# A planner that orders four engines: durations by kind, hops by engine, and dense weights in quarter rings

## The chip, the cores and the metric

One Trainium2 chip, one core. The metric is the device time of one execution in microseconds (us). The engines are named as the profile names them: PE (TensorE), DVE (VectorE), ACT (ScalarE), POOL (GpSimd) and SP (SyncE, which issues most transfers).

## What is computed

One layer of a diffusion backbone over 256 latent tokens and 256 context tokens of 2048 channels, in fp32. Cut to what matters:

```python
h  = modulate(rmsnorm(x, norm1_w), sh1, sc1)          # latent, 256 x 2048
hc = modulate(rmsnorm(ctx, norm1_w), csh1, csc1)      # context, 256 x 2048
rw, cv, z, ab, gt = split(h @ w_in)                   # the combined input projection; hc likewise
fa = rwkv_features(rw, grid_shift(rw), ...)           # 16 heads of 64: decay and iclr by low-rank products
out_a = [prefix_scan(rwkv7_scan, context, latent, s0, reverse) for both directions]
fb = gdn_features(cv, ab, conv_w, ...)                # 8 heads of 128: conv of 5 tokens, l2norm
out_b = [prefix_scan(gdn_chunked, context, latent, s0, reverse) for both directions]
m = sigmoid(g_a) * (o_a @ p_a) + sigmoid(g_b) * (o_b @ p_b)
x = x + gt1 * (m @ w_out)
x = x + gt2 * swiglu(modulate(rmsnorm(x, norm2_w), sh2, sc2), ...)
return rmsnorm(x, final_norm_w)
```

Both recurrences are computed in chunks of 64 tokens. Each needs the inverse of a triangular 64 x 64 matrix for each chunk, and a chain of small products that carries the state from chunk to chunk (8 steps for a pair of RWKV heads, context and latent, both directions at once; 4 steps of two chunks for a GDN head).

## The kernel before, in words

**Stages.** Until 133 us of the span the modulation vectors and norms are made. From 133 to 1368 us runs the woven stage: the input projection together with both recurrences. From 1368 us to the end the merge and the FFN run as plain products (`load_w`, `gemm`, L345 to L376). The change touches the woven stage alone.

**Dense products.** The input projection is 86 products of 128 output columns (`products`, L1061). Each takes its inputs in 16 blocks k of 128 channels, and each block is three matmuls, because fp32 is split in two parts: hi weight by hi input (`mm<-hxh,whi`), hi by lo (`mm<-hxl,whi`), lo by hi (`mm<-hxh,wlo`). They are 512 columns wide where the context is needed too, else 256. `cast` (L1041) loads the weights into two raw halves of 128 x 8 x 128 (512 KB each, tag wraw, 3 buffers), ACT makes the hi part of a quarter (`whi`, 128 x 512), DVE subtracts to get the lo part (`wlo`), and these go into a fixed ring of four quarters (L1037 to L1039). The ring's quarter is written again when the product before has read it.

**RWKV pairs.** `lowrank` (L733) makes decay and iclr inputs of the 8 pairs: for each pair four products `s<-lin,wraw`, whose outputs ACT takes through a sigmoid (`lo<-s`) and stores. For each two pairs it loads 384 KB of low-rank weights (`lora`) into a buffer of the tag wraw. Then for each pair come `prepare` (L765), `grams` (L847, whose helper `four` at L855 halves the planned cost of its products), `inverse` (L897), `values` (L908) and `scan` (L923). A step of the scan is a product `s<-VX,LA..`, a copy to R by ACT, a product `s<-R,Tx` with the inverse, copies to VX by ACT, and a product `s<-VX,KB` whose result DVE multiplies into VX for the next step.

**GDN heads.** `features`, `tokens`, `decays`, `head_grams`, `head_inverse` and `head_scan` (L1238 to L1377) for each of 8 heads. The inverse passes between engines and through memory: DVE ends a triangle, SP stores it (`tscr<-arena`), loads it back in another layout (`T<-tscr`), and DVE transposes it in blocks (`Tx<-T`). In the scan, DVE makes Vn from a product and the state St from the next. Beside the heads, `ada_rest` (L1449) makes the remaining modulation vectors on DVE: 180 steps `aw<-aw,ck`, each 128 x 512.

**What sets the order.** All pieces above are generators that yield operations. The planner (`Weave`, L170 to L266) runs them against a model of the engines while the program is built, and the order in which it takes operations is the order of the instructions on PE, DVE, ACT and POOL. It always takes the operation that can start first by its model, and between equals the one with the lower rank (scans low, dense products 900). The model is the table `LAT` (L30) and `Lane` (L112): a planned duration for each operation, `own` between two operations of a piece on the same engine, `hop` where the piece changes engines, `turn` where PE changes between dense (split) and other products, and `dma` behind a transfer. SP isn't planned; its transfers stand in the order in which the pieces ask for them, and each waits for its buffer in that order. Instructions of the planned engines all have line L143 in the profile, transfers L154.

Of the kernel before, what the change touches and what calls it, by code (L numbers as in the profile page):

```python
# [18 lines left out]
P = 128  # L19
D = 2048  # L20
KT = D // P
T = 256
# [7 lines left out]
LAT = dict(dma=2.4, v=1.0, s=1.0, hop=0.5, own=0.13, grp=32, crank=-1, cg=4, turn=0.09)  # L30
# [70 lines left out]

HOP = LAT['hop']


class Op:


    def __init__(self, lane, cost, call, split=False):
        self.lane, self.cost, self.call, self.split = lane, cost, call, split


class Lane:  # L112


    def __init__(self, engine, fixed, each, own):
        self.engine, self.fixed, self.each, self.own = engine, fixed, each, own

    def __getattr__(self, name):

        def op(out, *a, **k):  # L120
            if name == "preload_act_table_set":
                return Op(self, 1.3, lambda: self.engine.preload_act_table_set(out))
            if name == "dma_start":
                return Op(self, 0.6 if self.each > 0.002 else 0.06, lambda: self.engine.dma_start(out, *a))
            n = int(np.prod(out.shape[1:]))
            split = name == "matmul" and a[0].dtype == F32R
            if name == "transpose" and len(a) == 2:
                cost = 0.109
            elif split:
                cost = 0.0065 + 0.000443 * n  # L130
            elif name == "matmul":
                rows, m = a[0].shape[0], out.shape[0]
                if rows < 64:
                    cost = 0.009 if n <= 16 else 0.0125
                elif rows == 64:
                    cost = max(0.066, 0.027 + 0.0008 * n)
                elif rows < P or m == P:
                    cost = 0.0054 + 0.00167 * n
                else:
                    cost = 0.107  # L140
            else:
                cost = self.fixed + self.each * n
            return Op(self, cost, lambda: getattr(self.engine, name)(out, *a, **k), split)  # L143
        return op
# [24 lines left out]

class Weave:  # L170

    def __init__(self):
        self.work, self.free, self.done, self.now, self.split = [], {}, {}, 0.0, True

    def add(self, rank, gen, at=None):
        now = self.now  # L180
        w = [rank, gen, None, now if at is None else at, None, None]
        self.work.append(w)
        self.step(w, None)
        self.now = now

    def step(self, w, value):

        while True:
            self.now = w[3]
            try:  # L190
                x = w[1].send(value)
# [4 lines left out]
            if isinstance(x, float):  # L196
                w[3] += x
            w[5] = x if not isinstance(x, Op) else [x]
# [4 lines left out]
    def there(self, w):  # L203
        x = w[5]
# [4 lines left out]
    def take(self, w):  # L209
        x = w[5]  # L210
        w[5] = None
        if isinstance(x, tuple) and isinstance(x[0], Banks):
            w[3] = max([w[3]] + [b.free.pop(0) for b in x])
            return [b.tile() for b in x]
        if isinstance(x, Banks):
            w[3] = max(w[3], x.free.pop(0))
            return x.tile()
        w[3] = max(w[3], self.done[x] + HOP)

    def ready(self, *name):  # L220
        self.done[name] = self.now

    def release(self, banks):
        banks.free.append(self.now)

    def run(self):
        while self.work:
            for w in list(self.work):
                if w[5] is not None and not isinstance(w[5], (list, float)) and self.there(w):
                    self.step(w, self.take(w))  # L230
            best = None
            for w in self.work:
                if isinstance(w[5], float):
                    key = (w[3], w[0])
                    if best is None or key < best[0]:
                        best = (key, w, None)
                elif isinstance(w[5], list):
                    lane = w[5][0].lane
                    at = w[3] + (0.0 if w[4] is None else lane.own if w[4] is lane else HOP)
                    key = (max(self.free.get(lane, 0.0), at), w[0])  # L240
                    if best is None or key < best[0]:
                        best = (key, w, lane)
            if best is None:
                if any(w[5] is not None and not isinstance(w[5], (list, float)) and self.there(w) for w in self.work):
                    continue
                assert not self.work, [w[5] for w in self.work]
                return
            (start, _), w, lane = best
            if lane is None:
                w[5] = None  # L250
                assert w[3] < 1e5, [x[5] for x in self.work]
                self.step(w, None)
                continue
            ops, rest, w[4] = w[5], None, lane
            if lane is self.tensor:
                ops, rest = ops[:LAT['grp']], ops[LAT['grp']:]
                if ops[0].split != self.split:
                    start += LAT["turn"]
                self.split = ops[0].split
            w[5] = rest or None  # L260
            got = [o.call() for o in ops]
            w[3] = self.free[lane] = start + sum(o.cost for o in ops)
            if rest:
                w[4] = None
            else:
# [3 lines left out]
def emit(ctx: ExitStack, tc, A, out, dbg=None):  # L269
# [6 lines left out]
    e, v, s = Lane(E, 0.027, 0.00083, 0.0), Lane(V, 0.07 * LAT["v"], 0.00104 * LAT["v"], LAT["own"]), Lane(S, 0.06 * LAT["s"], 0.00086 * LAT["s"], LAT["own"])  # L276
    g = Lane(G, 0.06, 0.0024, LAT["own"])
# [441 lines left out]

    for b in (pib, mmb, psb, psb, mmb, pab):  # L720
# [4 lines left out]
    def lowrank_out(p, j, ps, so):  # L725
# [4 lines left out]
        if j == 3:  # L730
            weave.ready("lowrank", p)

    def lowrank():  # L733
# [17 lines left out]
        for p in range(NPAIR):  # L751
# [95 lines left out]
    def grams(p, d):  # L847
# [7 lines left out]
        def four(ops):  # L855
            for o in ops:
# [868 lines left out]
```

## Time and profile before

| | us |
|---|---|
| median of 3 runs | 2311.51 (2311.5 to 2324.71) |
| profiled execution, its own time | 2311.51 |
| its span, first instruction to last | 2309.7 |
| ahead of the woven stage | 133 |
| woven stage: low-rank products / RWKV scans / GDN heads / last dense products | 129 / 688 / 300 / 118 |
| merge and FFN | 941.7 |

The mean granted TensorE clock was 0.974. In a row of the profile, "a<-b,c" are the tiles written and read; "x4" after a shape counts instructions; what stands in square brackets or behind an arrow at the end is the idle time before it and what ended it. Dense matmuls overlap each other, so the distance between two starts (the pitch), not the duration, is what one costs.

### The profile page before, as it was taken

How to read it: one execution, taken by the hardware profiler on the slowest of the kernel's cores; microseconds unless marked ns; L12 is line 12 of the kernel's file. 1: busy time of each engine (PE TensorE's matmuls, PEld its weight loads, DVE VectorE, ACT ScalarE, POOL GpSimd, SP SyncE). 2: the span in 40 equal slices, each digit the busy share in tenths (PEclk: the TensorE clock that was granted, in tenths of full speed). 3: DMA queues.
4: the chain of work that ended last, by engine and by line, in shares of the span. 5: the costliest groups of instructions: out<-in, count | busy, mean ns of one | idle time of the engine just before them, and what ended most of it. 6: DMA issues, size and time to landing. Idle time of an engine off the chain costs nothing.

```text
span 2309.7 us, 54901 instructions
## 1 busy us (share of the span) xinstructions
PE 2176.4 (94%) x22904; PEld 1910.7 (83%) x22904; DVE 1553.1 (67%) x3242; ACT 1105.0 (48%) x2057; POOL 110.0 (5%) x183
## 2 busy tenths in 40 slices
PE   7988999999999999888888999999999999999998
PEld 4766677776778677776777989999999999999997
DVE  3447588887787558889988755765666666555554
ACT  3246554543555556544555446554444444444443
POOL 0000000000000001111111003000000000000000
PEclk9999999999999999999899999999999999999999
DMA  9956543443434236666667666663777776566665
GB/s 384 403 146 193 166 114 107 116 110 93 127 100 120 80 94 215 197 176 205 204 192 218 186 205 206 211 224 108 243 239 237 238 241 230 195 189 194 196 194 166
DMA packets 232728, 430.77 MB, mean 187 GB/s; under 512 B 114848, under 2 KB 130208, under 8 KB 228128
## 3 DMA queue, kind: packets, MB, share of 16 engines
q1 hardware_dynamic: 204832, 351.77, 48.8%
q0 software_dynamic: 13824, 50.34, 7.2%
q10 hardware_dynamic: 13824, 25.17, 3.3%
q8 instruction: 179, 2.93, 0.5%
q14 instruction: 69, 0.57, 0.1%
HBM read 401.44 MB, written 25.77 MB: 185 GB/s over the span
## 4 chain that ended last, share of the span: by engine, by line
PE 66%; DVE 15%; DMA 9%; ACT 5%; issue 4%; SPq 1%; ACTq 0%; DVEq 0%; POOL 0%; POOLq 0%
PE mm L143 17%; PE mm L376 12%; PE mm L374 12%; PE mm L375 12%; PE s L143 5%; DVE arena L143 4%; PE pa L143 3%; DVE aw L143 2%; DVE wlo L143 2%; DMA tscr<-arena 2%; PE pi L143 2%; DMA wr<-wgu 2%; PE mm L467 1%; DMA wraw<-wgu 1%; DVE wlo L365 1%
## 5 line engine op out<-in xcount | busy, mean ns | idle before, releaser
L365 DVE TENSOR_TENSOR wlo<-wraw,whi 128x1024 fp32r<-128x1024 f32 x328 | 393.3, 1199 | 340.6 <-ACT whi L364 339.7
L364 ACT CAST whi<-wraw 128x1024 fp32r<-128x1024 f32 x328 | 337.6, 1029 | 457.8 <-PE mm L375 403.0
L143 PE MATMUL mm<-hxh,wlo 128*128 128x256 f32 (+1 forms) x1376 | 470.1, 342 | 10.7 <-DVE wlo L143 10.1
L143 PE MATMUL mm<-hxh,whi 128*128 128x256 f32 (+1 forms) x1376 | 466.4, 339 | 4.8 <-ACT whi L143 4.6
L143 PE MATMUL mm<-hxl,whi 128*128 128x256 f32 (+1 forms) x1376 | 464.4, 338 | 0.0
L376 PE MATMUL mm<-hfh,wlo 128*128 128x256 f32 x1344 | 372.4, 277 | 1.3 <-DVE wlo L365 1.3
L374 PE MATMUL mm<-hfh,whi 128*128 128x256 f32 x1344 | 371.2, 276 | 0.0
L375 PE MATMUL mm<-hfl,whi 128*128 128x256 f32 x1344 | 371.2, 276 | 0.0
L143 PEld LDWEIGHTS mm<-hxh,wlo 128*128 128x128 f32 x1376 | 265.3, 193 | 39.3 <-DVE wlo L143 13.8
L143 DVE TENSOR_TENSOR wlo<-wraw,whi 128x512 fp32r<-128x512 f32 x344 | 238.0, 696 | 80.8 <-ACT whi L143 77.9
L143 PEld LDWEIGHTS mm<-hxh,whi 128*128 128x128 f32 x1376 | 266.1, 193 | 31.0 <-ACT whi L143 7.0
L143 PEld LDWEIGHTS mm<-hxl,whi 128*128 128x128 f32 x1376 | 265.8, 193 | 26.9 <-issue 5.0
L143 ACT CAST whi<-wraw 128x512 fp32r<-128x512 f32 x344 | 209.1, 617 | 137.9 <-PE mm L143 112.9
L376 PEld LDWEIGHTS mm<-hfh,wlo 128*128 128x128 f32 x1344 | 252.4, 188 | 2.9 <-DVE wlo L365 2.7
L374 PEld LDWEIGHTS mm<-hfh,whi 128*128 128x128 f32 x1344 | 252.5, 188 | 0.0
L375 PEld LDWEIGHTS mm<-hfl,whi 128*128 128x128 f32 x1344 | 252.5, 188 | 0.0
L374 PE MATMUL mm<-za,whi 128*128 128x256 f32 x512 | 141.5, 276 | 0.0
L376 PE MATMUL mm<-za,wlo 128*128 128x256 f32 x512 | 141.3, 276 | 0.0
L375 PE MATMUL mm<-za,whi 128*128 128x256 f32 x512 | 141.3, 276 | 0.0
L143 DVE SCALAR_TENSOR_TENSOR aw<-aw,ck 128x512 f32<-128x512 f32 x180 | 132.5, 749 | 3.3 <-DMA aw<-ada_rest 3.0
L143 DVE TENSOR_TENSOR arena<-arena 128x512 f32<-128x512 f32 (+17 forms) x522 | 121.3, 234 | 17.0 <-DMA arena<-scr 7.8
L375 PEld LDWEIGHTS mm<-za,whi 128*128 128x128 f32 x512 | 96.1, 188 | 0.0
(333 smaller groups left out, 3916.0 us busy)
## 6 DMA issues: line engine op xcount, KB each, us to landing
wraw<-w SPq DMA_DIRECT2D x172, 512.0 KB, 4.1
wraw<-wgu SPq DMA_DIRECT2D x168, 512.0 KB, 4.5
aw<-ada_rest POOLq DMA_DIRECT2D x96, 512.0 KB, 4.6
aw<-ada_first SPq DMA_DIRECT2D x32, 1024.0 KB, 12.0
wraw<-wdn SPq DMA_DIRECT2D x64, 448.0 KB, 3.7
wraw<-wout SPq DMA_DIRECT2D x32, 512.0 KB, 4.5
aw<-ada_gt ACTq DMA_DIRECT2D x64, 256.0 KB, 5.0
wraw<-wdn SPq DMA_DIRECT2D x32, 512.0 KB, 3.6
```

The costliest lines, as they stand in the source:

```text
L143: return Op(self, cost, lambda: getattr(self.engine, name)(out, *a, **k), split)
L364: S.copy(hi[:, c, :M], raw[:, c, :M])
L365: V.tensor_sub(lo[:, c, :M], raw[:, c, :M], hi[:, c, :M].bitcast(F32))
L374: E.matmul(ps, hi, Xh[:, k, :n], start=first and i == 0, stop=False)
L375: E.matmul(ps, hi, Xl[:, k, :n], start=False, stop=False)
L376: E.matmul(ps, lo, Xh[:, k, :n], start=False, stop=last and i == len(wt) - 1)
L467: E.matmul(ps[32 * g:32 * g + 32, 0:P], ckr[:, k].rearrange("p a b -> p (a b)"), aws[e, c][:, i, g], start=k == 0, stop=k == KT - 1)
```

## The change

**Planner.** A matmul's planned cost now depends on its kind (`product`), that of other engines on the operation and its operands (`cost`). Hops go by engine: PE 0.215, DVE 0.135, ACT 0.15, POOL 0.1, plus 0.1 of slack each, in place of 0.5 for all. `own` falls from 0.13 to 0.09 (0 on PE), `dma` rises from 2.4 to 3.1. PE is charged 0.14 for leaving the full array, 0.2 for coming back and 0.14 between two small kinds, where 0.09 stood for each change; 0.1 for a dense product after a pause; DVE and ACT 0.08 when the output's partitions change. A piece is an object that knows its own engine, so what it makes ready or releases counts from the end of its operation plus that engine's hop.

**Weights.** The rings of raw, hi and lo weights are quarters (128 x 4 x 128), handed out and given back one by one: 6 raw, 4 hi, 4 lo. `fetch` asks for a quarter (256 KB) when a raw one is free, `cast` splits it; each is a piece of its own. Until the low-rank products are done, two of the raw quarters are set aside for their weights, which are loaded per pair (192 KB) and two pairs ahead. `scan(0)` waits until the low-rank outputs of the last pair are done.

The core of the diff:

```diff
-LAT = dict(dma=2.4, v=1.0, s=1.0, hop=0.5, own=0.13, grp=32, crank=-1, cg=4, turn=0.09)
+LAT = dict(dma=3.1, v=1.0, s=1.0, hop=dict(e=0.215, v=0.135, s=0.15, g=0.1), slack=0.1, own=0.09, grp=32, crank=-1, cg=4, into=0.14, back=0.2, cross=0.14, stay=0.0)
...
+    def product(self, out, a):
+        n, rows, m = int(np.prod(out.shape[1:])), a[0].shape[0], int(np.prod(a[0].shape[1:]))
+        if a[0].dtype == F32R:
+            return 0.0065 + 0.000443 * n, "full"
+        if rows >= 96 and m == P:
+            return max(0.219, 0.012 + n * 4 / 2400), "full"
+        mode = (rows, m)
+        if rows < 64:
+            return 0.0165, mode
+        if rows == 64:
+            return (0.064 if n > 64 else 0.048) if m < P else 0.02 + n * 4 / 2400, mode
+        return (0.06 if m < 64 else 0.058), mode
...
+    def at(self, lane):
+        if self.lane is None:
+            return max(self.end, self.seen)
+        return max(self.end + (lane.own if lane is self.lane else self.lane.hop), self.seen)
+
+    def shown(self):
+        return max(self.end + (self.lane.hop if self.lane else 0.0), self.seen)
...
+    def turn(self, mode):
+        return 0.0 if mode == self.mode else LAT["back"] if mode == "full" else LAT["into"] if self.mode == "full" else LAT["cross"]
...
+    raws, his, los = quarters("wraw", 3, F32), Ring(quarters("whi", 2, F32R)), Ring(quarters("wlo", 2, F32R))
+    raws, spare = Ring(raws[:4]), raws[4:]
...
+    def lora(p):
+        landed["lora", p] = weave.now + dq(spare[p % 2][:96], A["lora"][p // 2, :, 4 * (p % 2):4 * (p % 2) + 4])
...
-            if p % 2 == 0:
-                w = wp.tile([P, 8, P], F32, tag="wraw", name="wraw", bufs=3)
-                yield dq(w[:96], A["lora"][p // 2])
+            if p == 0:
+                for i in range(2):
+                    lora(i)
+            yield max(0.0, landed["lora", p] - weave.now)
+            w = spare[p % 2]
             for j in (0, 2, 1, 3):
                 ps = yield psb
-                yield e.matmul(ps, w[:96, 4 * (p % 2) + j], lin[:, j], start=True, stop=True)
+                yield e.matmul(ps, w[:96, j], lin[:, j], start=True, stop=True)
                 weave.add(2, lowrank_out(p, j, ps, out[j]))
+            if p + 2 < NPAIR:
+                lora(p + 2)
+        raws.put(*spare)
...
-        if p:
-            yield "scan", p - 1
+        yield ("scan", p - 1) if p else ("lowrank", NPAIR - 1)
...
+    def fetch(src, i):
+
+        for q in range(NQ):
+            raw = yield raws
+            landed[i, q] = raw, weave.now + dq(raw, src[:, CG * q:CG * q + CG, :])
+            weave.ready("asked", i, q)
+            yield 0.0
+
+    def cast(i):
+
+        for q in range(NQ):
+            yield "asked", i, q
+            raw, at = landed.pop((i, q))
+            yield max(0.0, at - weave.now)
+            hi = yield his
+            yield s.copy(hi, raw)
+            lo = yield los
+            yield v.tensor_sub(lo, raw, hi.bitcast(F32))
+            raws.put(raw)
+            casts[i, q] = hi, lo
+            weave.ready("cast", i, q)
```

**Where instructions move.** PE, low-rank products of the later pairs (`s<-lin,wraw`; `pa<-C,arena` are transposes of the first pair; the rows `mm` are dense). Before:

```order
L143 MATMUL pa<-C,arena 128x128 x4
L143 MATMUL mm<-hxl,whi 128x512
L143 MATMUL s<-lin,wraw 128x512 x2
L143 MATMUL mm<-hxh,wlo 128x512
L143 MATMUL s<-lin,wraw 128x512 x6
L143 MATMUL mm<-hxh,whi 128x512
```

And now:

```order
L158 MATMUL s<-lin,wraw 128x512 x2
L158 MATMUL mm<-hxh,wlo 128x512
L158 MATMUL s<-lin,wraw 128x512 x2
L158 MATMUL pa<-LAl,arena 64x128 x16
L158 MATMUL s<-lin,wraw 128x512 x2
L158 MATMUL mm<-hxh,whi 128x512
L158 MATMUL s<-lin,wraw 128x512 x2
L158 MATMUL mm<-hxl,whi 128x512
L158 MATMUL s<-lin,wraw 128x512 x2
L158 MATMUL pa<-C,arena 128x128 x4
```

The products of six and eight in a row are taken apart into twos, with one other row between.

PE, a step of an RWKV scan, from the product with VX to the product with R. Before:

```order
L143 MATMUL s<-VX,LAc 64x64 x4
L143 MATMUL mm<-hxh,wlo 128x512
L143 MATMUL mm<-hxh,whi 128x512
L143 MATMUL mm<-hxl,whi 128x512
L143 MATMUL mm<-hxh,wlo 128x512
L143 MATMUL mm<-hxh,whi 128x512
L143 MATMUL s<-R_6133,Tx 64x64 x4
```

And now:

```order
L158 MATMUL s<-VX,LAl 64x64 x4
L158 MATMUL mm<-hxh,whi 128x512
L158 MATMUL mm<-hxl,whi 128x512
L158 MATMUL mm<-hxh,wlo 128x512
L158 MATMUL s<-R_6244,Tx 64x64 x4
L158 MATMUL s<-VX,C 64x128 x2
L158 MATMUL s<-LAl,VX 64x64 x4
```

Three dense matmuls stand where five stood, and the products that don't depend on R follow it directly.

DVE, third GDN head, from the last row of the triangle (`arena<-arena 64x15`) to the transpose of what was loaded back (`Tx<-T`). Before:

```order
L143 TENSOR_TENSOR arena<-arena 64x15 x2
L143 COPY arow<-pa 128x256
L143 SCALAR_TENSOR_TENSOR arena<-arena 128x256
L143 TENSOR_TENSOR arena<-s,arena 128x128 x2
L143 TENSOR_TENSOR mod<-pa,PR 128x4 x2
L143 TENSOR_TENSOR Qe<-Qe,arena 128x256
L143 TENSOR_TENSOR keg<-pa,egc 128x512
L143 TENSOR_TENSOR arena<-arena 128x256
L143 TENSOR_TENSOR kta<-pa,eta 128x512
L143 SCALAR_TENSOR_TENSOR arena<-arena,PR 128x256
L143 STREAM_TRANSPOSE Tx<-T_11590 128x256
```

And now:

```order
L158 TENSOR_TENSOR arena<-arena 64x15
L158 TENSOR_TENSOR keg<-pa,egc 128x512
L158 TENSOR_TENSOR wlo<-wraw,whi 128x512
L158 TENSOR_TENSOR kta<-pa,eta 128x512
L158 SCALAR_TENSOR_TENSOR aw<-aw,ck 128x512
L158 TENSOR_TENSOR keg<-pa,egc 128x512
L158 TENSOR_TENSOR wlo<-wraw,whi 128x512
L158 TENSOR_TENSOR kta<-pa,eta 128x512
L158 SCALAR_TENSOR_TENSOR aw<-aw,ck 128x512 x3
L158 TENSOR_TENSOR wlo<-wraw,whi 128x512
L158 TENSOR_TENSOR Qe<-Qe,arena 128x256
L158 SCALAR_TENSOR_TENSOR aw<-aw,ck 128x512
L158 STREAM_TRANSPOSE Tx<-T_11684 128x256
```

Between the two stand three `wlo`, five `aw` and five other instructions where eleven, most of them shorter, stood.

More of the change, by code (lines that the diff above doesn't have):

```diff
@@ L275, in emit @@
     dq = Loads(Q)
[L276 to L277 removed]
+    e, v, s, g = (Lane(x, fixed, each, LAT["own"], LAT["hop"][n]) for x, fixed, each, n in
+                  ((E, 0.0, 0.0, "e"), (V, 0.07, 0.00104, "v"), (S, 0.06, 0.0009, "s"), (G, 0.06, 0.0022, "g")))
+    e.own = 0.0
     ent = ctx.enter_context
@@ L713, in turn, with quarters @@
         weave.release(pab)
+    CG = LAT['cg']
+    NQ = KT // CG
+    def quarters(tag, n, dtype):
+        return [t[:, k:k + CG] for t in [wp.tile([P, 8, P], dtype, tag=tag, name=tag, bufs=n) for _ in range(n)] for k in range(0, 8, CG)]
+    raws, his, los = quarters("wraw", 3, F32), Ring(quarters("whi", 2, F32R)), Ring(quarters("wlo", 2, F32R))
+    raws, spare = Ring(raws[:4]), raws[4:]
     for b in (pib, mmb, psb, psb, mmb, pab):
@@ L1035, in gate_out, with weights @@
         Q.dma_start(gts_[j], g)
[L1037 to L1057 removed]
+    def fetch(src, i):
[16 more added lines that the diff above has]
+            weave.ready("cast", i, q)
+    def weights(src, i):
+        weave.add(LAT['crank'], fetch(src, i))
+        weave.add(LAT['crank'], cast(i))
     casts = {}
```

191 lines of the change are left out of this document (98 added, 93 removed).

## Prediction

> **What bounds the kernel now.** I read the page's busy times and the engine row of its chain first, then the windows of the stages, then the waits of PE and DVE inside a stage, and last the rows around single waits.
>
> From the page, the busy times, and by engine the chain that ended last:
>
> ```profile
> PE 2176.4 (94%) x22904; PEld 1910.7 (83%) x22904; DVE 1553.1 (67%) x3242; ACT 1105.0 (48%) x2057; POOL 110.0 (5%) x183
> ...
> PE 66%; DVE 15%; DMA 9%; ACT 5%; issue 4%; SPq 1%; ACTq 0%; DVEq 0%; POOL 0%; POOLq 0%
> ```
>
> PE is busy 94% of the span, and two thirds of the chain are PE. Time can be won only where PE stands still or works slowly. The windows say where (columns: window, its length, busy time of PE, weight loads, DVE, ACT and POOL, granted TensorE clock, DMA share, GB/s):
>
> ```profile
> 133.00:262.00 129.00, 113.56 (x801) 80.61 (x802) 77.95 (x172) 74.92 (x127) 2.30 (x6) 0.96 0.62 191
> 262.00:950.00 688.00, 660.46 (x8886) 519.92 (x8884) 531.06 (x1316) 352.12 (x840) 32.21 (x68) 0.98 0.43 119
> 950.00:1250.00 300.00, 257.75 (x2571) 211.35 (x2571) 267.25 (x650) 152.03 (x330) 51.05 (x83) 0.91 0.66 195
> 1250.00:1368.00 118.00, 115.09 (x1392) 109.66 (x1391) 82.99 (x230) 54.64 (x121) 2.68 (x4) 1.00 0.59 184
> ```
>
> The planner orders the instructions between 133 and 1368; the code ahead of that and behind it is left alone. PE is idle for 15.4, 27.5, 42.3 and 2.9 us in the four windows, 88.1 in all. They are four different situations. In the first (low-rank products) no engine is full. In the second (RWKV scans) PE is full and only 4% is left. In the third (GDN heads) DVE is busy 267 of 300 us, and PE waits for it. In the fourth PE has dense products only.
>
> What PE waits for in the first stage, then in the third, and what DVE waits for in the third (engine, tile, releaser: us in total, times, longest):
>
> ```profile
> PE mm L143 <- DVE wlo L143: 5.3, 6, 2.3
> PE s L143 <- DMA wraw<-lora: 4.3, 3, 1.7
> PE mm L143 <- ACT whi L143: 3.1, 4, 1.1
> PE s L143 <- ACT lo L143: 2.6, 1, 2.6
> ```
>
> ```profile
> PE s L143 <- DVE Vn L143: 6.8, 7, 1.9
> PE pa L143 <- ACT arena L143: 5.7, 3, 4.1
> ```
>
> ```profile
> DVE wlo L143 <- ACT whi L143: 8.7, 7, 3.0
> DVE Tx L143 <- DMA T<-tscr: 8.2, 3, 3.7
> ```
>
> In the first stage PE waits for dense weights (wlo, whi) and for the low-rank weights (lora). In the third the largest waits of DVE are for a cast on ACT and for the copy of an inverse through memory.
>
> **The change, part by part.** It leaves out no arithmetic: in the woven stage PE has 4128 dense and 4923 other matmuls in both orders, and DVE 2374 instructions. So each term is a change of waits or of turns.
>
> *Low-rank products.* Their weights are loaded two pairs ahead into two quarters of their own; they used to share the ring of the dense weights. These are the first and the second of the three stalls:
>
> ```profile
> 161.13 8.63 PE L143 MATMUL s<-lin,wraw 96*128 96x512 f32 x16 [1.37 <-DMA wraw<-lora]
> ...
> 217.43 8.61 PE L143 MATMUL s<-lin,wraw 96*128 96x512 f32 x16 [1.24 <-DMA wraw<-lora]
> ```
>
> Sixteen of these matmuls take 8.6 us, longer than any load quoted below, so a load that is asked for two pairs ahead has landed: the 4.3 us go. In the second group of pairs the new order puts dense matmuls between them in ones and twos, in place of clumps of 8, so the one wait for the eviction of lo (2.6) goes too. The waits for wlo and whi, 5.3 + 3.1 = 8.4, mostly belong to the narrow dense products at the start. There the changed order has 46 wide (512 columns) and 144 narrow (256 columns) dense matmuls ahead of the low-rank products, some 27 us at 0.23 and half of that a piece (the pitch of the rows at 609 below), where it had some 20. That is more cover, but the supply of weights is the same DVE and ACT; I take half, 4.2. Idle time: 4.3 + 2.6 + 4.2 = 11.1. The clock of the stage is 0.96, so 0.04 x 113.56 = 4.5 us of PE's work went to the lower clock; where gaps go I take half of it, 2.3. Sum **-13.4**; bounds -5 (lora and little else) and -19.9 (all 15.4 and all 4.5).
>
> *RWKV scans.* A hop between engines is now planned as 0.2 to 0.315 us (a value for each engine, plus 0.1) in place of 0.5, so PE comes back to a scan sooner. One step, PE and then ACT (six dense matmuls stand between the first row and the last):
>
> ```profile
> 604.65 0.45 PE L143 MATMUL s<-VX,LAc 128*64 128x64 f32 x8
> ...
> 605.38 0.39 PE L143 MATMUL mm<-hxh,wlo 128*128 128x512 f32 x1
> 605.61 0.39 PE L143 MATMUL mm<-hxh,whi 128*128 128x512 f32 x1
> ...
> 606.63 0.45 PE L143 MATMUL s<-R,Tx 64*64 64x64 f32 x8
> ```
>
> ```profile
> 605.78 0.25 ACT L143 COPY R<-s 128x128 f32<-128x128 f32 x1
> ```
>
> The copy ended at 606.03 and the second product started 0.6 us later. With three dense matmuls, 3 x 0.23 = 0.7 us less, it would come at 605.94 and wait 0.1 us. Counted over the 64 steps, 51 had five or more dense matmuls there and 6 had three or fewer; now 23 have five or more and 36 three or fewer. While PE is full, a shorter way through a scan wins nothing by itself; what can be won is part of the 27.5 us. Bounds: -14 (half of them) and +16, a wait of 0.15 us in each of 3 hops of 36 steps, 108 in all (half a mean DVE instruction of the window, 531.06/1316 = 0.40, by DVE's share of 0.77). In the step quoted the shorter cover is nearly enough, so I stay near zero: **-3**.
>
> *GDN heads.* DVE sets this stage. Its longest waits are for an inverse that goes through memory (SP's queue, then DVE, third head):
>
> ```profile
> 1007.23 0.59 SPq L154 DMA_DIRECT2D tscr<-arena  x1
> 1011.87 0.60 SPq L154 DMA_DIRECT2D T<-tscr  x1
> ```
>
> ```profile
> 1012.93 0.47 DVE L143 SCALAR_TENSOR_TENSOR arena<-arena,PR 128x256 f32<-128x256 f32 x1
> 1015.71 0.45 DVE L143 STREAM_TRANSPOSE Tx<-T 128x256 f32<-128x256 f32 x1 [2.30 <-DMA T<-tscr]
> ```
>
> From the store to the transpose 8.5 us pass; DVE had some 4 us of other work queued in between and then stood 2.3 us. The new order is made with 3.1 in place of 2.4 us for each transfer, and it queues three subtractions wlo, five steps of aw, two keg, two kta and a Qe there. By the rows of this window (kta as keg):
>
> ```profile
> L143 DVE SCALAR_TENSOR_TENSOR aw<-aw,ck 128x512 f32<-128x512 f32 x138 | 101.8, 752 | 2.4 <-DMA aw<-ada_rest 2.1
> L143 DVE TENSOR_TENSOR wlo<-wraw,whi 128x512 fp32r<-128x512 f32 x65 | 45.0, 695 | 8.7 <-ACT whi L143 8.7
> ...
> L143 DVE TENSOR_TENSOR keg<-pa,egc 128x512 f32<-128x512 f32 x10 | 6.8, 683 | 0.4 <-PE pa L143 0.4
> ...
> L143 DVE TENSOR_TENSOR Qe<-Qe,arena 128x256 f32<-128x256 f32 x10 | 4.2, 417 | 3.0 <-ACT Qe L143 2.8
> ```
>
> 3 x 0.695 + 5 x 0.752 + 4 x 0.683 + 0.417 = 9.0 us, a little more than the 8.5 of the way through memory. So the 8.2 us of waits for T go. Of the 8.7 us for whi I take half, 4.4, since a cast now needs only its own 256 KB. The clock of 0.91 gives nothing here, because PE isn't the engine that sets the end of this stage. What is late next is DVE's own work, which stays the same. Sum **-12.6**; bounds -32.8 (all of DVE's idle time, 300 - 267.25) and +5 (a filler too many, 0.7 us, ahead of each of the 7 waits for Vn).
>
> *Turns of the array.* Leaving the full array for small tiles and coming back costs what one excursion shows:
>
> ```profile
> 608.73 0.39 PE L143 MATMUL mm<-hxl,whi 128*128 128x512 f32 x1
> 609.05 0.45 PE L143 MATMUL s<-VX,KB 128*64 128x64 f32 x8
> 609.43 0.50 PE L143 MATMUL mm<-hxh,wlo 128*128 128x512 f32 x1
> 609.77 0.39 PE L143 MATMUL mm<-hxh,whi 128*128 128x512 f32 x1
> ```
>
> From 608.73 to 609.77 there are 1.04 us, of which two dense pitches (605.38 to 605.61) are 0.46 and the eight small products, by their 609.05 to 609.43 less a turn in, about 0.24; some 0.34 is the turn. Excursions fall from 288 to 283 and changes between small kinds from 85 to 81: 5 x 0.34 = 1.7, and between 0 and 4 x 0.34 for the others. I take **-2**.
>
> *Quarter loads.* 344 loads of 256 KB take the place of 172 of 512 KB. That is 172 issues more on SP, at 0.33 us 57 us, under SP's waits for buffers. SP's wait, one of its issues, the two sizes of load (median us to landing at the end), and the cast:
>
> ```profile
> SPq L154 <- DVE wlo L143: 312.5, 84, 23.1
> ```
>
> ```profile
> 1021.36 0.33 SPq L154 DMA_DIRECT2D wraw<-w  x1
> ```
>
> ```profile
> wraw<-w SPq DMA_DIRECT2D x172, 512.0 KB, 4.1
> ```
>
> ```profile
> arena<-sgd__1355 SPq DMA_DIRECT2D x32, 256.0 KB, 3.6
> ```
>
> ```profile
> L143 ACT CAST whi<-wraw 128x512 fp32r<-128x512 f32 x344 | 209.1, 617 | 137.9 <-PE mm L143 112.9 <-issue 9.9 <-DMA wraw<-w 9.5
> ```
>
> A quarter's turn is issue 0.33 + load 3.6 + cast 0.62 + subtraction 0.70 = 5.25 us. With six quarters one is ready every 0.88 us, with four (while the low-rank products run) every 1.31. It feeds 12 matmuls: 2.76 us of PE with wide products, half of that, 1.38, with narrow ones. So the cover is enough, and the edit costs **0**; without the cover it costs what rival (c) says.
>
> The Trainium skill, "DMA: Bandwidth & Descriptors", section "Bandwidth", speaks against this edit: it asks for transfers of at least 1 MiB. From the fixed 2.0 us per transfer that its section "Anatomy of one DMA" gives, at the rate fitted there, an estimate is 2.6 us for 256 KB and 3.2 for 512 KB. The trace's 3.6 and 4.1 show the same small difference, and the sum would be the same by either.
>
> Sum: -13.4 - 3 - 12.6 - 2 + 0 = -31.0. The profiled execution took 2311.51 us, which is also the median of the three runs, so the forecast is **2280.5 us**. The far bounds of the three larger terms lie 8, 19 and 20 us from their values; the root of their squares is 29, and 0.6 of it, 17, is taken for its own range: 2263 to 2298.
>
> **The rivals.** A measurement of this kernel can tell about 1%, 23 us, from no change: below 2288.4 is faster, above 2334.6 slower.
>
> (a) *Waits only move.* DVE is busy 89% in the third window and PE 96% in the second; a wait that goes can come back at the next instruction, with another name. For it: the work of both engines is fixed. Against it: the idle time of DVE in the third window is real, and longer than the waits that I take away. With the lora term (4.3) and the turns (2) alone: 2305.
>
> (b) *Hops too tight.* PE now returns to a scan after one shorter hop. If ACT or DVE is still in another operation, PE waits there, and every dense matmul is queued behind it. There are the 108 short hops of the RWKV scans and about 16 in each of 8 GDN heads: 236. For it: ACT was in another operation when R's product was done at 605, and PE waits for Vn already. Against it: the planner follows each engine's queue. At 0.25 us for each hop it costs 59 us: -31 + 59 = +28, 2339. It outweighs the gain from 31/236 = 0.13 us per hop on.
>
> (c) *Quarters late in the first window.* Another 256 KB load took longer:
>
> ```profile
> aw<-ada_gt ACTq DMA_DIRECT2D x64, 256.0 KB, 5.0
> ```
>
> With 5.0, four quarters turn in 6.65 us, one every 1.66, which is 0.28 too slow for narrow products. Some 28 narrow quarters stand ahead of the last low-rank product: +8, 2288.5. For it: the DMA share of 0.62 there; against it: the 3.6 of the sgd loads.
>
> (d) *More of the idle time goes.* If durations by kind make the plan come true, half of the 88.1 us goes, with half of the clock's loss in the first two windows, (4.5 + 0.02 x 660.46)/2 = 8.9, and the turns: -44 - 8.9 - 2 = -55, 2256.5. For it: clock and idle time go together, the clock being lowest, 0.91, where PE is idle most. Against it: in the third window DVE sets the pace.
>
> The Trainium skill, "TensorE: Matmul & The Clock Gate", section "HAM oscillation", puts a lowered clock down to gaps of PE of more than about 3.4 us. The trace shows a PE wait of 4.1 us in the window with 0.91; by that rule each such gap that goes returns clock as well, which is rival (d).
>
> **How the numbers follow.** Chances: the forecast 0.44, (a) 0.18, (b) 0.14, (c) 0.05, (d) 0.19. Faster by over 1%: 0.34 of the forecast, all of (d), 0.02 of (c): 0.55. Slower by over 1%: 0.13 of (b) and 0.01 of (a): 0.14. Within 1%: the rest, 0.31. The range 2242 to 2320 leaves out the far end of (d), 0.05, and 0.14 at the slow side; its low end is the sum of the forecast's turns with the opening's and GDN's idle time gone (2 + 15.4 + 32.8) and a further 19 of the RWKV window and of the clock.
>
> **What would show it.** Right: no PE waits for lora; PE idle some 4 us in the first window; no waits of Tx for T over 1 us, and the third window some 12 us shorter at the same busy time of DVE; PE's waits for R and VX in the scans as short as before. Wrong: waits of PE for ACT R, ACT VX and DVE Vn that sum to over 30 us (b); DVE idle as before, under other names (a); whi waiting for loads of weights in the first window (c).

## The result, and the profile after

The changed kernel takes 2288.3 us (median of 4 runs, 2285.7 to 2294.3), the kernel before 2316.4 (4 runs, 2311.5 to 2324.7). The ratio is 0.988, with an interval of 0.984 to 0.992: faster by 1.2%. The profiled execution took 2288.29 us, its span is 2286.5, 23.2 less than before.

From the page of the changed kernel, busy times, the chain by engine, and the loads of dense weights:

```profile
PE 2157.4 (94%) x22904; PEld 1905.4 (83%) x22904; DVE 1552.0 (68%) x3242; ACT 1110.6 (49%) x2062; POOL 112.8 (5%) x183
...
PE 76%; DMA 7%; DVE 6%; issue 5%; ACT 4%; POOL 1%; SPq 0%; DVEq 0%; ACTq 0%; POOLq 0%
...
wraw<-w SPq DMA_DIRECT2D x344, 256.0 KB, 3.3
```

The same 22904 matmuls are done. PE is busy 19.0 us less for them; its idle time (span less busy time) fell by 4.2 us alone, from 133.3 to 129.1. DVE is busy for as long as before, ACT and POOL a little longer. On the chain that ended last PE has 76% in place of 66%, and DVE 6% in place of 15%. Which stage gave the time can't be read from windows at fixed times, because the stages have moved. So I cut both traces at the same events: the last low-rank product, the last product with R of the RWKV scans, the last step of aw, and the first product with `w_out` (`mm<-mh`), which follows the merge. Windows of the kernel before, cut there, then of the changed one (columns as in the prediction):

```profile
133.00:254.80 121.80, 106.36 (x642) 74.29 (x643) 75.01 (x166) 70.93 (x120) 2.30 (x6) 0.97 0.62 190
254.80:851.40 596.60, 574.02 (x8239) 447.21 (x8237) 450.31 (x1110) 299.73 (x732) 16.77 (x44) 0.97 0.39 105
851.40:1267.70 416.30, 368.77 (x3524) 307.09 (x3521) 368.64 (x911) 215.95 (x461) 68.09 (x110) 0.93 0.67 200
1267.70:1472.60 204.90, 195.05 (x2048) 187.67 (x2047) 129.85 (x282) 108.48 (x209) 22.28 (x17) 0.98 0.62 199
```

```profile
133.00:248.00 115.00, 102.28 (x625) 74.85 (x626) 72.19 (x161) 69.36 (x119) 1.99 (x6) 0.94 0.64 194
248.00:834.70 586.70, 568.77 (x8243) 445.67 (x8241) 451.30 (x1112) 301.49 (x734) 16.95 (x44) 0.97 0.41 108
834.70:1251.50 416.80, 367.46 (x3561) 308.73 (x3556) 371.88 (x921) 217.96 (x465) 70.25 (x110) 0.93 0.68 203
1251.50:1453.20 201.70, 190.28 (x2025) 184.03 (x2024) 127.81 (x280) 112.51 (x210) 23.05 (x17) 0.98 0.61 197
```

The stages took 6.8, 9.9 and 3.2 us less, and the GDN stage 0.5 more. The code that follows, which the change leaves alone, took 3.8 us less (833.3 against 837.1); over all kernels below it varies from 833 to 839, so I read nothing into that.

One correction is needed. Dense matmuls can be done in any stage, so a stage is shorter also when it leaves dense work to a later one. Below, "less dense" is the time of a stage minus its dense matmuls (in the last stage with those of the merge, `mm<-oah` and `mm<-oal`, which follow there), counted in the trace, at their pitch of 0.229 us (512 columns) or 0.1145 (256). On that measure the stages I (low-rank), II (RWKV) and III + IV (GDN heads and what follows up to the last event) went from 61.4, 294.0 and 253.8 us to 58.4, 283.3 and 247.9.

### The profile page after: what moved, and what is told of

Read it like the earlier page. It is cut to its first block, busy times and chain, and to the rows that moved or that the text cites. A ratio compares the mean times of both kernels' runs of the same rounds, so it can differ in the third digit from the quotient of the medians.

```text
span 2286.5 us, 55426 instructions
## 1 busy us (share of the span) xinstructions
PE 2157.4 (94%) x22904; PEld 1905.4 (83%) x22904; DVE 1552.0 (68%) x3242; ACT 1110.6 (49%) x2062; POOL 112.8 (5%) x183
## 4 chain that ended last, share of the span: by engine, by line
PE 76%; DMA 7%; DVE 6%; issue 5%; ACT 4%; POOL 1%; SPq 0%; DVEq 0%; ACTq 0%; POOLq 0%
PE mm L158 24%; PE mm L429 12%; PE mm L431 12%; PE mm L430 12%; PE s L158 7%; PE pa L158 4%; DMA aw<-ada_rest 2%; PE pi L158 2%; DMA wr<-wgu 1%; DVE arena L158 1%; PE mm L522 1%; DVE aw L158 1%; DVE wlo L158 1%; DVE wlo L420 1%; DMA wraw<-w_low 1%
## 6 DMA issues: line engine op xcount, KB each, us to landing
aw<-ada_first SPq DMA_DIRECT2D x32, 1024.0 KB, 11.4
```

## The experiments

Each kernel was timed beside the kernel before on the same chip; there it took 2317.0, 2319.4 and 2318.0 us in the three groups (E1 to E4, E5 to E8, E9 to E12). Where an edit is to one entry of the table LAT, only that entry is shown. An order that the planner writes from one set of numbers is called a draw.

The last three columns are the "less dense" times, in us, of one profiled execution each. That execution lay up to 11 us from the median of its kernel (E11 took 2302.7 in it, E12 2323.8), so 10 us in one column of one row aren't told from noise.

| | kernel | us, median | ratio to before (95%) | I | II | III + IV |
|---|---|---|---|---|---|---|
| | before | 2316.4 | | 61.4 | 294.0 | 253.8 |
| | changed | 2288.3 | 0.988 (0.984 to 0.992) | 58.4 | 283.3 | 247.9 |
| E1 | changed, hops at 0.5 | 2313.3 | 0.997 (0.995 to 0.999) | 56.0 | 284.7 | 271.5 |
| E2 | changed, weights in halves | 2299.2 | 0.992 (0.989 to 0.995) | 64.7 | 264.3 | 261.7 |
| E3 | changed, lora not ahead | 2331.5 | 1.006 (1.004 to 1.009) | 69.2 | 286.8 | 279.3 |
| E4 | changed, slack 0.11 | 2320.6 | 1.001 (1.000 to 1.003) | 59.3 | 282.4 | 276.8 |
| E5 | before, hop 0.49 | 2318.1 | 1.000 (0.998 to 1.002) | 62.9 | 300.9 | 242.5 |
| E6 | before, hop 0.51 | 2306.7 | 0.994 (0.992 to 0.996) | 60.2 | 285.7 | 258.3 |
| E7 | changed, slack 0.09 | 2329.5 | 1.004 (1.003 to 1.006) | 60.1 | 273.0 | 293.1 |
| E8 | changed, slack 0.12 | 2305.2 | 0.994 (0.993 to 0.996) | 59.5 | 275.7 | 267.5 |
| E9 | before, hop 0.25 | 2297.6 | 0.990 (0.988 to 0.993) | 63.5 | 283.5 | 250.8 |
| E10 | changed, aw row 5.0 | 2311.9 | 0.997 (0.995 to 0.999) | 58.1 | 279.5 | 268.0 |
| E11 | changed, dma 2.4 | 2313.9 | 0.998 (0.996 to 1.000) | 56.1 | 276.8 | 270.8 |
| E12 | changed, dma 2.4, slack 0.11 | 2312.7 | 0.998 (0.996 to 1.000) | 60.2 | 286.3 | 274.2 |

### E1: hops as before

```diff
-hop=dict(e=0.215, v=0.135, s=0.15, g=0.1), slack=0.1
+hop=dict(e=0.4, v=0.4, s=0.4, g=0.4), slack=0.1
```

> The changed kernel with every hop planned at 0.5 us again (0.4 plus the slack of 0.1); everything else as changed. Against the kernel before, the changed one reached the last R product of the RWKV scans 16.7 us earlier, 9.9 of it after the low-rank products. Theory 1, the shorter planned hops made the scans shorter: the gain of the scans goes, the time is about 2300 us, and the median number of dense matmuls between VX and R products goes back to five or six. Theory 2, the weights in quarters made it (fewer waits for whi and wlo): stays at 2288 within 6 us. Theory 3, any new order moves the time by some 10 us either way: no forecast of the sign.

It took 2313.3 us. The scan steps did what theory 1 says: from a step's last VX product to its first R product the median was 1.64 us before, 1.05 in the changed kernel and 1.51 here, and the median number of dense matmuls in between was 6, 3 and 5. The second stage took 596.9 us, 10 more than in the changed kernel. But less dense it was 284.7, as short as there (283.3): it only held more dense work. The loss is in III + IV. So neither theory 1 nor theory 2 gives the time; one run can't separate an edit from the order that it redraws, as E4 shows.

### E2: weights in halves again

```diff
...
-        for q in range(NQ):
+        for c in range(2):
             raw = yield raws
-            landed[i, q] = raw, weave.now + dq(raw, src[:, CG * q:CG * q + CG, :])
-            weave.ready("asked", i, q)
+            at = weave.now + dq(raw, src[:, 8 * c:8 * c + 8, :])
...
-            raws.put(raw)
+            if q % 2:
+                raws.put(full)
```

> The changed kernel with dense weights loaded in halves of 512 KB again (three raw halves, two until the low-rank products end), a half given back after its second cast; hi and lo stay rings of quarters and the planner is the changed one. Theory 1 (hops): within 6 us of the changed kernel, 2282 to 2294. Theory 2 (quarters): about 2300 to 2305, with longer waits of the casts for loads. The page's rule that larger transfers are better would give a gain of 0.5 us of latency per load, at most a few us in the first window.

It took 2299.2 us, 11 more than the changed kernel. The first stage is 6 us longer, less dense: 64.7, where the eight draws with quarters and prefetch (the changed kernel, E1, E4, E7, E8, E10 to E12) have 56.0 to 60.2. ACT's waits for loads there in the changed kernel, then in E2:

```profile
ACT whi L158 <- DMA wraw<-w: 6.2, 5, 4.2
```

```profile
ACT whi L158 <- DMA wraw<-w: 8.6, 4, 4.0
```

These waits aren't what makes the difference: with quarters they are 12.2 us in E12, at 60.2. The second stage was the shortest of all less dense (264.3), III + IV longer. As far as one draw tells, quarters are worth those 6 us in the first stage at most, for a reason that isn't shown; the rest is within what a redrawn order does (E4).

### E3: low-rank weights not ahead

```diff
...
-            if p == 0:
-                for i in range(2):
-                    lora(i)
-            yield max(0.0, landed["lora", p] - weave.now)
+            if p % 2 == 0:
+                yield dq(third[:96], A["lora"][p // 2])
...
-            if p + 2 < NPAIR:
-                lora(p + 2)
```

> The changed kernel with the low-rank weights loaded for two pairs at once (384 KB) when the pair before has been planned, not ahead; the two quarters set aside stay. Prediction's term: three stalls of PE for lora, 4.3 us in all, come back, and PE's products before the last low-rank one end some 4 us later: 2292. Rival: PE's waits in this stage only take another name (the changed kernel has 2.9 us on a store of gates and 1.1 on lora there), so it stays at 2288 within 3 us.

The first stage grew by 10.8 us less dense (58.4 to 69.2), more than twice what was expected, and the kernel took 2331.5. PE's waits there, in the changed kernel and in E3:

```profile
PE mm L158 <- DVE wlo L158: 4.4, 4, 2.0
PE pa L158 <- DMA gts__1373<-arena: 2.9, 1, 2.9
...
PE s L158 <- DMA wraw<-lora: 1.1, 1, 1.1
PE s L158 <- ACT lo L158: 0.7, 3, 0.3
```

```profile
PE mm L158 <- DVE wlo L158: 4.9, 6, 2.0
PE s L158 <- ACT lo L158: 4.7, 4, 3.4
PE s L158 <- DMA wraw<-lora: 2.7, 2, 1.9
```

Waits for lora came back (2.7), and with them those for the eviction of lo (4.7), both of which the prediction had named; together they grew by 5.6 us, about half of the 10.8. So the changed kernel needs its prefetch in this stage. How much of the gain over the kernel before is due to it isn't shown: E3 keeps the two quarters set aside, and is slower here than the kernel before (61.4), whose loads of these weights could go into any of three halves. Of the 43 us that E3 loses, 31 are in III + IV, where a redrawn order alone loses nearly as much (E4).

### E4: a slack of 0.11 us

```diff
-slack=0.1
+slack=0.11
```

> The changed kernel with a slack of 0.11 us in place of 0.10: a change of 0.01 us in each planned hop that by itself should be worth nothing. Theory 1 and 2: 2288 within 3 us. Theory 3 (the order is redrawn, and with it which waits come out): a difference of 5 us or more, of either sign; it would then be the yardstick for what one edit of the planner's numbers shows.

2320.6 us: one hundredth of a microsecond in the plan cost 32 us, more than the whole change had won. Stages I and II are as before the edit (59.3 and 282.4 less dense). The loss is in the GDN heads, as four stalls of PE, one in each of four heads. One of them, on PE and then on ACT:

```profile
1022.11 1.79 PE L158 MATMUL pa<-arena 128*128 128x128 f32 x12
1033.05 2.08 PE L158 MATMUL pa<-arena,CR 128*128 128x512 f32 x2 [9.14 <-ACT arena L158]
```

```profile
1028.49 1.28 ACT L158 ACT_TABLE_LOAD   x1 [5.43 <-DVE arena L158]
1029.79 1.27 ACT L158 ACTIVATE arena<-arena 128x1280 f32<-128x1280 f32 x1
1031.07 1.28 ACT L148 ACT_TABLE_LOAD   x1
1032.37 0.63 ACT L158 ACTIVATE arena<-arena 128x512 f32<-128x512 f32 x1
```

The norm sum of a head's features (`pa<-arena,CR`) stands next on PE. It needs a Silu, and that needs the convolution on DVE, which ends at 1028.4 with other DVE work between its steps. Behind it come two loads of ACT's tables, 1.28 us each, and two ACT operations, 4.5 us in all. The order has no dense matmul in between, so PE stands for 9.1 us. The window says what else that does:

```profile
832.00:1264.10 432.10, 364.51 (x3431) 298.93 (x3427) 369.92 (x892) 212.44 (x452) 67.80 (x112) 0.89 0.64 193
```

DVE is busy for as long as in the changed kernel (369.9 against 371.9) in a window that is 15 us longer, and the granted clock is 0.89 in place of 0.93. The Trainium skill, "TensorE: Matmul & The Clock Gate", section "HAM oscillation", says that PE gaps of over about 3.4 us lower the clock; here the window with five such gaps, these four and one of 3.9, has the lower clock.

### E5 and E6: the kernel before with hops of 0.49 and 0.51

```diff
-hop=0.5
+hop=0.49
...
-hop=0.5
+hop=0.51
```

> The kernel before with a planned hop of 0.49 us in place of 0.50 and nothing else. Theory 3 (every redrawn order moves the time, mostly through the GDN heads): 5 us or more away from the kernel before, either way. Rival, theory 4 (the old planner's order is steady, only the new planner's is not): within 4 us of the kernel before, 2313 to 2321.

> The kernel before with a planned hop of 0.51 us. As for 0.49: theory 3 expects 5 us or more away from 2317, theory 4 within 4 us. With the two and the kernel before there are three draws of the old planner to set against the draws of the new one.

2318.1 and 2306.7 us. The old planner's order is redrawn too, and one of the two moved by 13 us; theories 3 and 4 each got one of the two. In III + IV the three orders of the old planner have 242.5 to 258.3 less dense, with DVE idle for 43 to 48 us in stage III; E1 to E4 have 261.7 to 279.3 less dense.

### E7 and E8: slack 0.09 and 0.12

```diff
-slack=0.1
+slack=0.09
...
-slack=0.1
+slack=0.12
```

> The changed kernel with a slack of 0.09 us in place of 0.10. With 0.11 it took 32 us longer, in four stalls of PE of 6 to 9 us, one in each of four GDN heads. Theory 3: somewhere from 2285 to 2325, and the RWKV scans (last low-rank product to last R product) at 574 to 587 us all the same, since they were that long in all draws with short hops. Rival, theory 5 (0.10 is a true optimum, and a smaller slack gives tighter hops, which PE pays for): over 2310, lost in waits of PE for R, VX and Vn.

> The changed kernel with a slack of 0.12 us. Theory 3: anywhere from 2285 to 2325, with no order along 0.09, 0.10, 0.11, 0.12. Theory 5: over 2320, more than with 0.11, since PE comes back later and later.

2329.5 and 2305.2 us. There is no order along 0.09, 0.10, 0.11, 0.12: 2329.5, 2288.3, 2320.6, 2305.2. Theory 5 falls: with 0.09, PE's waits for R in the scans were 0.7 us, and the scans were among the shortest (273.0, and 564.5 us as they stand, less than the 574 to 587 expected). It lost in the GDN heads, where PE waited for these two things:

```profile
PE pa L158 <- ACT arena L158: 29.4, 10, 8.4
PE pa L158 <- DVE LT L158: 15.7, 2, 8.8
```

Both are the stall of E4 again: the five gaps of more than 5 us in this stage (8.4, 7.7, 8.8, 6.9 and 5.8) all stand ahead of norm sums (`pa<-arena,CR`), and where the profile names LT, ACT had ended its last operation 0.02 us before. Theory 3 stands, though 2329.5 lies above its 2325: four plans that differ by 0.03 us spread over 41 us, and the spread is made after the scans.

### E9: one part alone, hops of 0.25 in the kernel before

```diff
-hop=0.5, own=0.13
+hop=0.25, own=0.13
```

> The kernel before with one part of the change alone: hops planned at 0.25 us in place of 0.50, all other planned numbers, rings and loads as before. Stage by stage (last low-rank product; from it to the last R product; from that to the last aw step), three draws of the old planner took 121 to 124, 588 to 597 and 416 to 420 us; four of the new one 115 to 117, 565 to 587 and 417 to 442. Theory 1 (short hops make the scans shorter): the second stage falls to 575 to 585 us, the first stays at 121 to 124, and the total is near 2305 if the third stage stays at 416 to 420. Rival: the scans gain from the durations by kind and the turns, not from the hops: the second stage stays at 588 to 597 us. If the third stage grows to 430 or more, short hops are also what costs in the GDN heads.

2297.6 us, 0.990 (0.988 to 0.993) of before. One number in the old table gave 20 us, where the whole change gave 28; like all rows it is one draw, and E6 won 13 with a longer hop. Its windows, cut at the same events:

```profile
133.00:251.40 118.40, 105.01 (x617) 72.86 (x618) 71.36 (x160) 69.76 (x117) 2.90 (x6) 0.94 0.62 189
251.40:818.00 566.60, 549.57 (x8062) 424.89 (x8060) 433.90 (x1083) 289.37 (x706) 17.29 (x43) 0.98 0.39 104
818.00:1234.10 416.10, 375.04 (x3580) 309.41 (x3575) 369.10 (x907) 217.82 (x469) 73.17 (x111) 0.96 0.67 205
1234.10:1461.40 227.30, 213.88 (x2193) 206.02 (x2193) 143.04 (x322) 120.15 (x229) 23.03 (x17) 0.97 0.59 188
```

The scans end 33 us earlier than before (818.0 against 851.4) and the time from VX to R is 1.05 us as in the changed kernel. Nearly 20 us of that is dense work handed on, which the last window does later (227.3 in place of 204.9); 10.5 is won (294.0 to 283.5). The stage is shorter than the 575 to 585 us of theory 1. The third window is as long as before, so in this draw short hops cost nothing in the GDN heads.

### E10: a longer planned load for aw

```diff
-            yield 3.5
+            yield 5.0
```

> The changed kernel with the planned time of a row load of aw, a constant 3.5 us, raised to 5.0 us (the loads land after 4.7 us). In the GDN heads DVE waits for these loads 11.2 us in the changed kernel, 8 to 13 in its other draws, 3 to 5 in draws of the old planner. Theory 6 (waits of Tx were only exchanged for waits of aw): DVE's waits for aw in this stage fall to under 5 us, and the stage gets some 6 us shorter but for what the redrawn order does. Rival: the aw rows are limited by their transfers, so the waits stay at 8 or more whatever the plan says.

DVE's waits for aw fell to 4.0 us, as theory 6 said:

```profile
DVE Tx L158 <- DMA T<-tscr: 10.0, 3, 5.3
...
DVE aw L158 <- DMA aw<-ada_rest: 4.0, 6, 1.8
```

But its waits for T rose to 10.0, and PE waited 24.5 us for T. The third stage got 51 us longer, the fourth 31 shorter, and the kernel took 2311.9. The rival that the rows can't come in time falls; the gain that theory 6 hoped for can't be seen in one draw.

### E11 and E12: transfers planned at 2.4 us again

```diff
-LAT = dict(dma=3.1
+LAT = dict(dma=2.4
```

> The changed kernel with the planned time of a transfer at 2.4 us again (3.1 in the change). Prediction's term: with 2.4 DVE's waits for T in the GDN heads come back, to 10 us or more from 4.6 us. Rival: they stay at 5 to 8, since they depend on what happens to stand in the order. Total: anywhere from 2285 to 2325 by theory 3.

> The changed kernel with transfers at 2.4 us and a slack of 0.11. A second draw for the same question: waits of DVE for T 10 us or more if 2.4 brings them back, 5 to 8 if not; and whether the stalls of PE ahead of the norm sums of four heads (6 to 9 us each with a slack of 0.11) belong to the slack: they stay if they do, and go if any redrawn order can lose them.

2313.9 and 2312.7 us. DVE's waits for T in the GDN heads, E11 and then E12:

```profile
DVE Tx L158 <- DMA T<-tscr: 10.3, 6, 2.5
```

```profile
DVE Tx L158 <- DMA T<-tscr: 17.2, 5, 5.0
```

With 3.1 us they were 4.5 us in the changed kernel and 4.6 with the slack of 0.11; both draws with 2.4 have 10 or more, as the prediction's mechanism asks. The other draws with 3.1 have 0.8 to 10.0 (E1 the least, E7 9.3, E10 the most), and those of the old planner, with 2.4, 9.7 to 13.2 but for the 4.2 of E9. So the longer time helps but doesn't settle it. In E12 the stalls of E4 ahead of the norm sums are gone, with the same slack: they belong to the draw. Others of about 6 us stand ahead of products of the inverse.

## Why the prediction was right, and where its working wasn't

The forecast was 2280.5 us and faster; 2288.3 lies in its own range of 2263 to 2298. The size is near, the way to it was not: the three larger terms are 7 to 10 us off each, and that these errors partly cancel is luck. The terms came out as follows in the profiled executions, less dense.

| term | predicted | measured |
|---|---|---|
| low-rank products (stage I) | -13.4 | -3.0 |
| RWKV scans (II) | -3 | -10.7 |
| GDN heads and what follows (III + IV) | -12.6 | -5.9 |
| turns, not separated from the others | -2 | |
| code that isn't changed | 0 | -3.8 |
| sum | -31.0 | -23.4 |

Waits that go were to bring some 27 of the 31 us. PE's idle time over the span fell by 4.2 us; from 133 us on, in the four windows cut at events, it went from 95.4 to 91.4. The rest of the gain is shorter busy time for the same matmuls, which the forecast had only in the clock of the first stage and in the turns. Of the five signs that were to show it right none came out whole: PE waits 1.1 us for lora, is idle for 12.7 in the first window, one wait for T is 3.9 long, the GDN window is no shorter, and PE's waits for R and VX grew a little:

```profile
PE s L143 <- ACT VX L143: 0.9, 3, 0.4
PE s L143 <- DVE VX L143: 0.9, 3, 0.4
...
PE s L143 <- ACT R L143: 0.6, 2, 0.5
```

```profile
PE s L158 <- ACT R L158: 2.3, 3, 1.2
PE s L158 <- DVE VX L158: 2.0, 1, 2.0
PE s L158 <- ACT VX L158: 1.0, 3, 0.5
```

**Low-rank products.** The waits for lora fell from 4.3 to 1.1 us and those for lo from 2.6 to 0.7, nearly as forecast. Those for wlo and whi fell by 2.9 of the 4.2 (5.5 left). What failed is the step from waits to time: a store of gates now stands in the way for 2.9 us, PE's idle time fell from 15.4 to 12.7 us and not to 4, and the clock of the window is 0.94, not higher. E3 says, in one draw, that the new rings need the prefetch: without it 10.8 us are lost.

**RWKV scans.** The step that failed is "while PE is full, a shorter way through a scan wins nothing by itself". The changed kernel's step, PE and then ACT:

```profile
586.58 0.67 PE L158 MATMUL s<-VX,LAc 128*64 128x64 f32 x8
...
587.96 0.45 PE L158 MATMUL s<-R,Tx 64*64 64x64 f32 x8
```

```profile
587.34 0.27 ACT L158 COPY R<-s 128x128 f32<-128x128 f32 x1 [1.40 <-PE s L158]
```

1.38 us lie between the products here, with five dense matmuls in between, four of them narrow: the cover of three wide ones. The copy ended at 587.61, 0.35 ahead of the second product. So the cover was enough: rival (b) is excluded, as PE's waits for ACT R and ACT VX in the scans and for Vn in the GDN heads (3.4) sum to 6.7 us, where it asks for over 30.

The stage is 10.7 us shorter less dense, and 10.5 in E9. Of E9's gain 5.6 us is PE's idle time (22.6 to 17.0, from the windows); the remainder is busy time of PE beyond the dense pitch. In the changed kernel the two parts are 4.7 and 6.0. The second part goes with the hops: from the start of a small product to the start of the next small one, waits over 0.15 us left out, PE spends 172.9 to 176.1 us of this stage in the four profiles with hops near 0.5 (before, E1, E5, E6) and 163.4 to 170.7 in the ten with short hops, for some 6100 such steps in each. Why small products follow each other faster there I haven't separated. The stage as a whole doesn't go with the hop so clearly: E6, whose hop is longer than before, has 285.7. Of seven draws of the changed planner with short hops that keep its rings and prefetch (the changed kernel, E4, E7, E8, E10 to E12) the mean of stage II is 279.6, against 293.5 for three of the old planner with hops near 0.5. That gap of 14 is the part of the gain that holds over the draws. It isn't all the hop: E1, with hops at 0.5 in the new planner, has 284.7.

**GDN heads.** The waits for T fell, as E11 and E12 also say, and the gain was handed on. DVE's waits in the changed kernel, same window as above:

```profile
DVE aw L158 <- DMA aw<-ada_rest: 11.0, 12, 2.2
DVE wlo L158 <- ACT whi L158: 9.7, 12, 1.8
DVE Tx L158 <- DMA T<-tscr: 4.5, 2, 3.9
```

In the kernel before they were, cut at the same events:

```profile
DVE wlo L143 <- ACT whi L143: 11.7, 10, 3.0
DVE Tx L143 <- DMA T<-tscr: 11.3, 4, 3.7
DVE arena L143 <- DMA arena<-scr: 4.3, 2, 2.7
DVE aw L143 <- DMA aw<-ada_rest: 3.0, 3, 1.7
```

The steps of aw that fill the way of the inverse through memory are planned as if their own rows landed after 3.5 us (4.7 measured), and here they are late: 6.8 us less for T, 8.0 more for aw. E10, which plans 5.0, has 4.0 for aw. DVE is idle for 44.9 us in this window, against 47.7 before. That is rival (a), in this stage. Of the 4.4 us for whi 2.0 came.

**What the forecast missed.** The delivered plan is a lucky one. The changed planner's numbers with a slack of 0.09 to 0.12 take 2310.9 us on average over four, the old planner with hops of 0.49 to 0.51 takes 2314 over three. All the draws of the new planner except the delivered one have 262 to 293 us in III + IV, the four of the old one 242 to 258. So the new planner wins some 14 us in the scans and gives up about 20 in the GDN heads, on average; the delivered kernel alone, with 247.9, has the first without the second. Part of the reason is shown. Ahead of the norm sums PE stands for 44.4 us in stage III of E7, 31.7 in E4, 18.4 in E10 and 15.8 in E8, and for 2.8 to 11.4 in the other ten. Less these waits, III + IV has 245 to 252 us in those four, much as in the old planner's draws (240 to 253); E1 to E3, E11 and E12 still have 257 to 271. Waits for aw don't decide it: the changed kernel has 11.0 us of them, E11 1.9 and 270.8 in III + IV. Which of the new planned costs makes the orders of the GDN heads worse stays open. With one draw for each edit and a spread of 41 us from the slack alone, no such experiment could have shown it.

**Turns and quarters.** The 2 us for turns can't be seen beside this. The quarters cost nothing that can be seen, as forecast: a load of 256 KB lands in 3.3 us (4.1 for 512 KB before), and with halves again (E2) the first stage is 6 us longer. The sign of rival (c) did show: ACT's casts wait 6.2 us for loads in the first window (the line is under E2), where before they waited 2.5:

```profile
ACT whi L143 <- DMA wraw<-w: 2.5, 1, 2.5
```

But its price of 8 us didn't come, as PE's waits for wlo and whi fell. That its total of 2288.5 is the measured time is chance. Rival (d) is excluded: it asks for half of the idle time, 44 us.

## What to carry to other kernels

Where a planner writes the order, an edit to its numbers is a new draw as well as a change; move a number by a hundredth that should mean nothing, both ways, before believing a gain of 1%. Cut traces at events, and take movable work out of each stage, or a stage seems to win what it only handed on. A wait that is filled moves to whatever the filler needs: look at the filler's own loads first. The old planner with short hops and the prefetch wasn't tried; by E9 and E3, one draw each, it would be the next kernel to build.

## What the runs showed of the hardware

In this kernel long gaps of PE and a lower granted clock go together. Counted in stage III with the length quoted under E4, six profiles have none to two gaps of over 3.4 us and a clock of 0.92 to 0.96 (before, changed, E2, E5, E6, E9); the other eight have three to five and 0.88 to 0.91. A gap needn't be much longer for it: the longest is 3.9 us in E1 and 9.1 in E4, and both have 0.89.

A load of dense weights of half the size was 0.8 us shorter, so a quarter pays most of a half's time. It isn't a rule: the loads of lora, cut from 384 to 192 KB, took 4.8 us in place of 3.6.
